# Layer 0's modulation parts 2 to 5: from the head of the work queue to single steps spread among other products

## The chip, the cores and the metric

The kernel runs on one core of a Trainium2 chip. The metric is device time in microseconds (us), here the median of three runs. The core has five engines that each execute their own instruction list in order and wait for each other by semaphores: TensorE (PE, the matrix products, with a second track PEld for loading its stationary operand), VectorE (DVE), ScalarE (ACT), GpSimd (POOL) and SyncE (SP), which issues most of the transfers from memory. Matrix products accumulate in eight banks of PSUM.

## The reference

Two layers (DEPTH = 2) of a diffusion backbone over 256 latent and 256 context tokens, width 1024. Each layer modulates a normalised input by vectors that come from a small product, mixes tokens in three parallel branches, merges them through gates, and runs a gated MLP:

```
def modulation(cvec, w_mod, b_mod):
    m = jax.nn.silu(cvec) @ w_mod + b_mod
    return jnp.split(m[..., None, :], 6, axis=-1)
...
xn = adaln(x, norm1[l], m_lat[0], m_lat[1])
y_lat, y_ctx = token_mixer(xn, hn, ...)        # latent attention, windowed attention, gated delta net
x = x + m_lat[2] * y_lat
x = x + m_lat[5] * conv_ffn(adaln(x, norm2[l], m_lat[3], m_lat[4]), ...)
...
def merge(gates, ya, yb, yc, w_pa, w_pb, w_pc, w_out):
    ga, gb, gc = jnp.split(jax.nn.sigmoid(gates), 3, axis=-1)
    return (ga * (ya @ w_pa) + gb * (yb @ w_pb) + gc * (yc @ w_pc)) @ w_out
```

So parts 0 and 1 of the modulation are needed at once, part 2 only after the output projection, 3 and 4 for the second norm, 5 at the layer's end.

## The kernel before

Both token sets are stacked to 512 columns. Every weight block of 512 KB is loaded into one of three `raw` buffers, split by ScalarE (`wh`, line 189) and VectorE (`wl`, line 179) into a high and a low half, and multiplied in three passes (`mm3`, lines 199 to 201). A unit of `linear` is 256 output columns: two PSUM tiles of 24 products each, in two loads. The tiles come from the tag `mm`, which has three banks (`NMM`); everything else uses the tag `g` with five.

A modulation part (`mod_part`, line 578) is 8 loads of 512 KB, used straight from `raw` with no split: per load 4 matmuls (line 593) into one `mm` tile that stays open for the whole part, and after every second load a yield. So a step is 1 MB and 8 matmuls, a part four steps. Behind the last step the tile is copied out (line 598), transposed (line 601) and added to the bias (line 603). Parts 0 and 1 of layer 0 run at the start of the kernel; layer 1's six run in layer 0's MLP.

The order of layer 0's mixer is set by a queue of generators. A serial chain (the gated delta net's tables, decay, solve and scan; later the two attentions) yields a number at each point where PE would wait for it; `fill` adds the number to a credit, capped at 12, and takes steps from the head of the queue until the credit is used up, each step costing what it yields:

```
self.credit = min(self.credit + us, self.P["cap"])
while self.credit > 0 and self.queue:
    us = next(self.queue[0])
    self.credit -= us
```

The queue is first [q part, v part, kv, gates], later [z, modulation parts 2 and 3] ahead of the gates (`push` puts generators ahead of them), and for the attentions [rotary steps of the windowed attention `gsp`, modulation parts 4 and 5, gates]. A modulation step costs 4.0 in the first place and 0.9 in the second (`modc`). `finish` runs a generator to its end with no credit. The gates are last in the queue: 12 units whose sigmoids go to memory (line 1373) and are read back at the merge (line 1511). A gate unit that has not run when the attentions end is computed in the merge itself (line 1529). A build-time scheduler then sets the final order on each engine, near the order of the calls; `high_priority` moves some of them ahead.

Names that the prediction uses: line 839 is `times_k` (products of keys) in the decay, 877 the first block of the solve, 935, 951, 965, 980 the scan; 1014 the scan's output transposes; 1047, 1094 and 1110 scores, transposes and values of both attentions, 1084 their normalisation; 1248 to 1252 the rotary steps of the windowed attention and 1264 the cast of its keys; 662, 665 and 667 the three reads that take a convolved tile out of its bank; 671 the activation after them and 688 its transposes; 1372 the gates' sigmoid; 1359 z.

Of the kernel before, what the change touches and what calls it, by code (L numbers as in the profile page):

```python
# [29 lines left out]
def make_consts():  # L30
# [56 lines left out]
MARK = None  # L87
P = dict(pw=4,
    l1={}, s2=(2, 1, 2, 0), pe=(0.0, 0.1, 0.0, 0.0), ov=0, np=(0.1, 0.0, 0.25, 0), ly=2, qs=(0, 4), dec1=3.0, dec2=4.0, sol1=4.2, sol2=4.0,
    sol3=1.0, sol4=2.0, sca=(1.0, 2.0), scb=(1.0, 2.0), scc=(1.0, 2.0),   cap=12.0, sl=(0.3, 0.3, 0.5, 0.1), modc=(4.0, 0.9),  # L90
    lag=(0, 0, 2, 4, 5), nmod=(2, 5), hk=(5, 12), f0=(1.0, 1.6, 1.0, 1.0, 1.5, 1.0, 1.0), f1=(1.0, 1.0, 1.0, 0.3, 1.0, 1.0, 0.3), lat=1.0,
    bx=4, wd=0, dc=1, gk=(0, 0), hpe=60, w_t=5, w_k=3, w_s=0, w_r=1.5, w_n=3, w_o=4.0, nr=3, nh=3, nl=4, nb2=7, st=0, ab=(0.0, 0.0, 0.0, 0.0),
    st2=6, bge=2, hpa=40, hpn=0, hpk=40, hpv=40)

_INS = ["x", "c", "ctx", "c_ctx", "w_mod", "b_mod", "norm1", "norm2", "w_in", "mla_q_norm", "mla_kv_norm",
# [39 lines left out]
class Kernel:  # L135
# [67 lines left out]
    def run_gen(self, g):  # L203
        for us in g:
            self.wait = us if isinstance(us, Lat) else 0.0
            self.ahead()
            self.gcount += 1
            if self.bg and self.gcount % self.bg_every == 0:
                try:
                    next(self.bg[0])  # L210
                except StopIteration:
                    self.bg.pop(0)

    def fill(self, us, burst=0.0):

        self.credit = min(self.credit + us, self.P["cap"])
        if self.credit < burst:
            return
        while self.credit > 0 and self.queue:
            if self.wait > 0 and self.queue[0] is not self.gates:  # L220
                self.ahead(1)
            if self.credit <= 0 or not self.queue:
                continue
            try:
                us = next(self.queue[0])
                if isinstance(us, Lat):
                    self.wait = us * self.P["lat"]
                else:
                    self.credit -= us
            except StopIteration:  # L230
                self.queue.pop(0)

    def bg_steps(self):

# [348 lines left out]
    def mod_part(self, l, part, room="raw"):  # L583
# [5 lines left out]
        for k in range(KD):  # L589
            t = self.b4([128, D]) if room == "s4" else self.sb([128, D], "raw", F32, self.NRAW)  # L590
            nc.sync.dma_start(out=t, in_=i["w_mod"][l, k * 128:k * 128 + 128, part * D:part * D + D])
            for q in range(4):
                nc.tensor.matmul(ps[q * 32:q * 32 + 32, :256], lhsT=self.cT[:, k, :], rhs=t[:, q * 256:q * 256 + 256],
                                 start=k == 0, stop=k == KD - 1, tile_position=(0, q * 32))
            if k % 2:
                yield self.modcost
        ev = self.b2([128, 256])
        nc.vector.tensor_copy(ev, ps[:, :256])
        pt = self.ps([128, 4, 128], tag)
# [693 lines left out]
    def layer(self, l):  # L1293
# [113 lines left out]
        self.run_gen(self.gdn_misc(l, X))  # L1407
        gq, gv, gkv, gcq, gsq, gz = self.gdn_part(l, X, 0), self.gdn_part(l, X, 2), proj_kv(), proj_cq(), proj_sq(), proj_z()
        gmk, gmq, go0, go1, gsp = self.mla_kv(l), self.mla_q(l), self.gdn_out(l, 0), self.gdn_out(l, 1), self.swa_prep(l)
        mods = [self.modulation(l, 1), self.modulation(l, 2)]  # L1410
        self.gates = self.gates or gates()
        self.queue = [gq, gv, gkv, self.gates]
        spill = self.dram.tile([128, KD, T], F32, name=f"spill{l}")
# [11 lines left out]
        chain(self.gdn_decay(1, has_q[1]), f=P[f"f{l}"][2])  # L1425
        self.mark(f"gscan_{l}_0")
        alloc_zsq()
        push(*([gz, mods[0]] if l == 0 else [gz, gsq, gcq]))
        if has_q[0]:
            for tl in range(2):  # L1430
                self.times_k(0, tl, 1, self.qk[0][:, tl])
# [25 lines left out]
        nh = 8 // len(qh)  # L1457
        snk = self.sm([128, 8])
        nc.sync.dma_start(out=snk, in_=i["swa_sink"][l].partition_broadcast(128))
        if l == 0:  # L1460
            for _ in self.load_vectors(1):
                pass
            for j in range(DEPTH):
                self.load_conv(j)
        push(*([gsp, mods[1]] if l == 0 else [gsp]))
        self.modcost = self.P["modc"][1]
        ga = self.attend(streams, lambda h: ((qh[h // nh][:, h % nh, :], kh[h // 4][:, h % 4, :]),),
                         lambda h, kt: vt[kt // 2][:, kt % 2, h * 64:h * 64 + 64], lambda u: A["qrs"][:, self.q(u[0] * S, T).start // 128 + u[2]:][:, 0:1], None, False, ya, self.P["sl"][2 * l])
        hs = lambda h: slice((h // 4) * 64, (h // 4) * 64 + 64)
# [24 lines left out]
            self.queue.remove(self.gates)  # L1494
        self.gates = None
        self.finish(*list(self.queue))
        self.modcost = self.P["modc"][0]
        self.tap(f"ya{l}", ya)
        self.tap(f"yb{l}", yb)
        self.tap(f"yc{l}", yc)  # L1500
# [14 lines left out]
        for bi, ((gi, b), y) in enumerate(zip(gate_br, (yc, ya, yb))):  # L1515
# [4 lines left out]
            for u in range(4):  # L1520
# [16 lines left out]
                        nc.gpsimd.tensor_tensor(out=mt, in0=mt, in1=sg[t], op=ALU.add)  # L1537

                self.run_gen(self.linear(i["w_branch_" + b][l], 0, 4, u * 256, 256, yy, ev, cols=lambda _: slice(0, n)))
        self.mark(f"wout_{l}")  # L1540
        mh = [[self.s8([128, 4, n], F32R) for _ in range(2)] for _ in range(2)]
        mH, mL = [[mh[j][k // 4][:, k % 4] for k in range(KD)] for j in range(2)]
# [98 lines left out]
    def run(self):  # L1641
        nc, tc, i = self.nc, self.tc, self.ins
        self.NS8, self.NS4, self.NB2, self.NSM = 8, 9, self.P["nb2"], 32
        self.NRAW, self.NWH, self.NWL, self.NMM = self.P["nr"], self.P["nh"], self.P["nl"], 3
        self.queue, self.bg, self.gcount, self.bg_every, self.credit, self.modcost, self.gates, self.wait, self.sq_last, self.bgx, self.unit, self.wide = [], [], 0, 3, 0.0, 4.0, None, 0.0, None, None, 0, False
        with tc.tile_pool(name="per", bufs=1) as self.per, tc.tile_pool(name="sb", bufs=1) as self.pool, \
                tc.tile_pool(name="psum", bufs=1, space=PSUM) as self.psum, \
                tc.tile_pool(name="dram", bufs=1, space=DRAM) as self.dram:
            self.setup()
            for l in range(DEPTH):  # L1650
                self.layer(l)
            self.mark("final")
            self.final()
# [62 lines left out]
```

## Time and profile before

| | us |
|---|---|
| median of 3 runs | 1779.97 (1774.64 to 1780.54) |
| profiled execution, its own time | 1780.76 |
| span of its instructions | 1779.0 |
| PE, records of matmuls | 1679.0 (94%) |
| VectorE busy | 1133.4 (64%) |
| ScalarE busy | 769.2 (43%) |
| GpSimd busy | 300.4 (17%) |
| mean granted PE clock | 0.968 of full |

Busy PE means that a matmul's record is open. At half clock the records are longer, so a stretch can read as fully busy and still lose time; the granted clock beside it tells. The profile follows one execution, and a wait for several semaphores is put down to the one that came last.

### The profile page before, as it was taken

To read this page: it belongs to the slowest core of one execution; us is meant where nothing else is said; L and a number is where in the kernel's file an instruction comes from. 1 tells how busy PE (TensorE), PEld (TensorE's weight loads), DVE (VectorE), ACT (ScalarE), POOL (GpSimd) and SP (SyncE) were. 2 spreads that over 40 slices of the span, in tenths; PEclk is the share of its full clock that TensorE was granted. 3 is DMA by queue.
4 is the path that set the end of the run, shared out by engine and by line. 5 is a ranking of instruction groups with operands and counts; after the bars stand their busy time and mean duration, and the time that the engine had idled before them with its cause. 6 is when DMAs were issued, how large, how long until landed. Compare 5 with 4: busy or idle time off the path is not lost. (4 is left out here: it accounts for less than half of the span.)

```text
span 1779.0 us, 31557 instructions
## 1 busy us (share of the span) xinstructions
PE 1679.0 (94%) x12723; PEld 1363.7 (77%) x12723; DVE 1133.4 (64%) x2159; ACT 769.2 (43%) x1371; POOL 300.4 (17%) x281
## 2 busy tenths in 40 slices
PE   7989988999999999999999999999898899999997
PEld 4768765776556888768888888778787667999997
DVE  3897595474865643545535553699796776677684
ACT  3644312233755333324313432464523475555463
POOL 1040411221200222001100112030502310213010
PEclk8999998998999999999999999999998999999999
DMA  9423326333043633663333343434352223745663
GB/s 346 115 72 107 96 73 190 72 75 111 25 143 122 210 119 120 253 231 96 98 95 103 95 141 120 125 92 141 90 120 58 60 77 98 236 144 182 185 185 124
DMA packets 216944, 228.75 MB, mean 129 GB/s; under 512 B 51228, under 2 KB 195422, under 8 KB 215646
## 3 DMA queue, kind: packets, MB, share of 16 engines
q1 hardware_dynamic: 211582, 220.11, 40.5%
q10 hardware_dynamic: 4928, 6.56, 1.0%
q8 instruction: 100, 1.64, 0.4%
q14 instruction: 46, 0.38, 0.1%
q0 software_dynamic: 288, 0.06, 0.0%
HBM read 213.85 MB, written 11.80 MB: 127 GB/s over the span
## 5 line engine op out<-in xcount | busy, mean ns | idle before, releaser
L179 DVE TENSOR_TENSOR wl<-raw,wh 128x1024 fp32r<-128x1024 f32 (+2 forms) x294 | 364.3, 1239 | 250.2 <-ACT wh L189 248.6
L189 ACT CAST wh<-raw 128x1024 fp32r<-128x1024 f32 (+2 forms) x294 | 298.4, 1017 | 422.3 <-PE mm L200 220.5
L199 PE MATMUL mm<-xnh,wh 128*128 128x512 f32 (+2 forms) x1072 | 380.3, 356 | 5.8 <-ACT wh L189 2.4
L201 PE MATMUL mm<-xnh,wl 128*128 128x512 f32 (+2 forms) x1072 | 375.9, 353 | 1.3 <-DVE wl L179 1.3
L200 PE MATMUL mm<-xnl,wh 128*128 128x512 f32 (+2 forms) x1072 | 376.0, 351 | 0.1
L199 PEld LDWEIGHTS mm<-xnh,wh 128*128 128x128 f32 (+1 forms) x1072 | 206.3, 193 | 39.4 <-issue 7.0
L201 PEld LDWEIGHTS mm<-xnh,wl 128*128 128x128 f32 (+1 forms) x1072 | 205.9, 192 | 31.5 <-issue 3.3
L200 PEld LDWEIGHTS mm<-xnl,wh 128*128 128x128 f32 (+1 forms) x1072 | 206.1, 192 | 27.8 <-issue 2.9
L199 PE MATMUL g<-xnh,wh 128*128 128x256 f32 (+1 forms) x496 | 167.3, 340 | 1.4 <-ACT xnh L405 1.4
L200 PE MATMUL g<-xnl,wh 128*128 128x256 f32 (+1 forms) x496 | 166.4, 337 | 0.2 <-DVE xnl L406 0.2
L201 PE MATMUL g<-xnh,wl 128*128 128x256 f32 (+1 forms) x496 | 166.1, 336 | 0.0
L201 PE MATMUL mm<-s,wl 128*128 128x256 f32 (+1 forms) x458 | 150.0, 328 | 0.6 <-DVE wl L179 0.6
L199 PE MATMUL mm<-s,wh 128*128 128x256 f32 (+1 forms) x458 | 150.1, 329 | 0.4 <-DVE s L534 0.3
L200 PE MATMUL mm<-s,wh 128*128 128x256 f32 (+1 forms) x458 | 149.6, 327 | 0.1
L1616 POOL TENSOR_TENSOR b<-b,b 128x512 f32<-128x512 f32 (+1 forms) x44 | 54.3, 1234 | 442.5 <-DVE b L1600 381.6
L199 PEld LDWEIGHTS g<-xnh,wh 128*128 128x128 f32 x496 | 94.6, 192 | 15.0 <-issue 3.3
L199 PE MATMUL g<-s,wh 128*128 128x512 f32 (+1 forms) x304 | 102.8, 338 | 0.0
L201 PEld LDWEIGHTS g<-xnh,wl 128*128 128x128 f32 x496 | 94.6, 191 | 10.5 <-issue 1.2
L200 PEld LDWEIGHTS g<-xnl,wh 128*128 128x128 f32 x496 | 94.7, 191 | 10.1 <-DVE xnl L406 0.8
L200 PE MATMUL g<-s,wh 128*128 128x512 f32 (+1 forms) x304 | 102.2, 336 | 0.0
L201 PE MATMUL g<-s,wl 128*128 128x512 f32 (+1 forms) x304 | 102.2, 336 | 0.0
L199 PEld LDWEIGHTS mm<-s,wh 128*128 128x128 f32 x458 | 87.2, 191 | 8.8 <-DVE s L534 1.1
(285 smaller groups left out, 2743.6 us busy)
## 6 DMA issues: line engine op xcount, KB each, us to landing
raw<-in_w_in_dram SPq DMA_DIRECT2D x92, 512.0 KB
raw<-in_ffn_up_dram SPq DMA_DIRECT2D x80, 512.0 KB
s<-in_w_mod_dram SPq DMA_DIRECT2D x64, 512.0 KB
raw<-in_w_mod_dram SPq DMA_DIRECT2D x32, 512.0 KB
raw<-in_ffn_down_dram SPq DMA_DIRECT2D x32, 512.0 KB
raw<-in_w_out_dram SPq DMA_DIRECT2D x16, 512.0 KB
raw<-in_ffn_down_dram SPq DMA_DIRECT2D x16, 384.0 KB
spill<-s SPq DMA_DIRECT2D x4, 1024.0 KB
```

Source lines behind the costliest of these rows:

```text
L179: self.nc.vector.tensor_tensor(out=out, in0=x, in1=h.bitcast(F32), op=ALU.subtract)
L189: nc.scalar.copy(H, raw)
L199: mm(ps, lhsT=wH, rhs=xH, start=start, stop=False)
L200: mm(ps, lhsT=wH, rhs=xL, start=False, stop=False)
L201: mm(ps, lhsT=wL, rhs=xH, start=False, stop=stop)
L1616: nc.gpsimd.tensor_tensor(out=y[:, cs], in0=y[:, cs], in1=av[t][:, cs], op=ALU.mult)
```

## The change

The two generators for parts 2 and 3 and for 4 and 5 of layer 0 no longer stand in the queue. They form a list of their own, `drip`. Every product step that yields, in the queue or run to its end by `run_gen`, adds its yield to a counter (`drop`); at 14.0 the counter is reset and one modulation step is taken, which costs 1.0 of credit. What is left when the merge is done is run before the output projection.

```
-    scc=(1.0, 2.0),   cap=12.0, sl=(0.3, 0.3, 0.5, 0.1), modc=(4.0, 0.9),
+    scc=(1.0, 2.0),   cap=12.0, sl=(0.3, 0.3, 0.5, 0.1), modc=1.0,
...
-    bx=4, wd=0, dc=1, ...
+    bx=4, drip=14.0, wd=0, dc=1, ...
...
         for us in g:
             self.wait = us if isinstance(us, Lat) else 0.0
             self.ahead()
+            self.drop(us)
...
                     self.credit -= us
+                    self.drop(us)
...
+    def drop(self, us, every=None):
+
+        self.dropped += us
+        if self.drip and self.dropped >= (self.P["drip"] if every is None else every):
+            self.dropped = 0.0
+            try:
+                self.credit -= next(self.drip[0])
+            except StopIteration:
+                self.drip.pop(0)
...
             if k % 2:
-                yield self.modcost
+                yield self.P["modc"]
...
-        mods = [self.modulation(l, 1), self.modulation(l, 2)]
+        if l == 0:
+            self.drip = [self.modulation(l, 1), self.modulation(l, 2)]
...
-        push(*([gz, mods[0]] if l == 0 else [gz, gsq, gcq]))
+        push(*([gz] if l == 0 else [gz, gsq, gcq]))
...
-        push(*([gsp, mods[1]] if l == 0 else [gsp]))
-        self.modcost = self.P["modc"][1]
+        push(gsp)
...
+        while self.drip:
+            self.drop(0.0, 0.0)
         self.mark(f"wout_{l}")
```

In the new program the lines behind the change have other numbers: 593 is 605, 980 is 992, 935 is 947, 1084 is 1096, 1251 and 1252 are 1263 and 1264, 1264 is 1276.

On PE, in the scan of group 0 behind the last z product (`mm_2232`), the order before was this, with scan blocks (lines 965, 980, 935) between the modulation's matmuls:

```order
L201 MATMUL mm_2232<-xnh_227,wl_2272 128x512
L593 MATMUL mm_2347<-raw_2348,cT 32x256 x4
L593 MATMUL mm_2347<-raw_2354,cT 32x256 x4
L965 MATMUL g_2364<-b_351_2360,s_45_263 64x64 x8
L965 MATMUL g_2374<-b_351_2360,s_45_263 64x64 x8
L593 MATMUL mm_2347<-raw_2390,cT 32x256 x4
L980 MATMUL g_2404<-b_357_2402,s_142_769 64x64 x16
L935 MATMUL g_2422<-b_328_2152,s_49_267 64x64 x3
L593 MATMUL mm_2347<-raw_2396,cT 32x256 x4
```

In the changed program the last z product there (`mm_2376`) is followed by gate products (`mm_2516`), with one step of 8 modulation matmuls among them:

```order
L201 MATMUL mm_2376<-xnh_227,wl_2440 128x512
L199 MATMUL mm_2516<-xnh_227,wh_2520 128x512
L200 MATMUL mm_2516<-xnl_228,wh_2520 128x512
L201 MATMUL mm_2516<-xnh_227,wl_2521 128x512
...
L605 MATMUL mm_1580<-raw_2530,cT 32x256 x4
L605 MATMUL mm_1580<-raw_2536,cT 32x256 x4
L199 MATMUL mm_2516<-xnh_227,wh_2520 128x512
L200 MATMUL mm_2516<-xnl_228,wh_2520 128x512
```

Two whole parts in a row have become one step, and gate products have taken their place. The tile `mm_1580` of part 3 had been opened long before.

On GpSimd, in the latent attention, the rotary steps of the windowed attention (lines 1251 and 1252) stood between the attention's normalisations (line 1084) before:

```order
L1084 TENSOR_SCALAR b_623_4158<-b_623_4158,sm_4144 128x256
L1251 TENSOR_TENSOR s_238_1398<-s_238_1398,cst 128x256
L1252 TENSOR_TENSOR s_238_1398<-s_238_1398,b_636_4191 128x256
L1251 TENSOR_TENSOR s_544_3783<-s_544_3783,cst 128x256
L1252 TENSOR_TENSOR s_544_3783<-s_544_3783,b_649_4225 128x256
L1084 TENSOR_SCALAR b_646_4216<-b_646_4216,sm_4197 128x256
```

In the changed program they come behind the last of those normalisations, the one of 512 columns, and the casts of the keys (line 1276) behind them all:

```order
L1096 TENSOR_SCALAR b_744_4674<-b_744_4674,sm_4655 128x256
L1096 TENSOR_SCALAR b_808_4862<-b_808_4862,sm_4857 128x512
L1263 TENSOR_TENSOR s_245_1435<-s_245_1435,cst 128x256
L1264 TENSOR_TENSOR s_245_1435<-s_245_1435,b_847_5012 128x256
L1263 TENSOR_TENSOR s_593_4110<-s_593_4110,cst 128x256 x2
L1264 TENSOR_TENSOR s_593_4110<-s_593_4110,b_849_5018 128x256
...
L1264 TENSOR_TENSOR s_593_4110<-s_593_4110,b_855_5036 128x256
L1276 CAST s_858_5047<-s_858_5047 64x512 x2
```

All ten rotary instructions and the two casts now form one block at the boundary of the two attentions.

## Rows read from the trace of the kernel before

**Rows 1.** The page, part 1: busy us, share of the span, instructions.
```profile
PE 1679.0 (94%) x12723; PEld 1363.7 (77%) x12723; DVE 1133.4 (64%) x2159; ACT 769.2 (43%) x1371; POOL 300.4 (17%) x281
```

**Rows 2.** Busy by stretch: length, busy by engine (instructions), granted clock, DMA share, GB/s.
```profile
64.80:85.90 21.10, 20.81 (x103) 16.35 (x101) 18.23 (x57) 11.21 (x20) 0.00 (x0) 1.00 0.33 81
85.90:190.40 104.50, 98.68 (x485) 79.44 (x485) 78.86 (x158) 49.20 (x92) 21.27 (x18) 0.97 0.32 95
190.40:219.70 29.30, 28.82 (x413) 22.02 (x412) 17.92 (x21) 11.38 (x16) 20.66 (x17) 1.00 0.32 94
219.70:304.10 84.40, 69.26 (x963) 50.83 (x962) 61.51 (x131) 15.84 (x23) 8.28 (x8) 0.90 0.42 133
304.10:388.00 83.90, 80.99 (x1089) 62.07 (x1088) 46.82 (x90) 26.16 (x42) 17.71 (x19) 0.96 0.29 69
388.00:433.60 45.60, 39.84 (x195) 30.30 (x196) 23.28 (x57) 12.09 (x22) 9.59 (x9) 0.94 0.32 80
433.60:564.10 130.50, 123.98 (x676) 75.56 (x676) 94.08 (x282) 89.40 (x229) 14.64 (x17) 0.94 0.30 96
564.10:674.90 110.80, 110.80 (x498) 90.63 (x497) 53.00 (x59) 34.44 (x46) 23.19 (x15) 1.00 0.51 168
```

**Rows 3.** Waits from 219.7 to 304.1: who waited for whom, us, times, longest.
```profile
PEld mm L593 <- DMA raw<-in_w_mod_dram: 7.2, 8, 1.5
PE mm L593 <- DMA raw<-in_w_mod_dram: 5.8, 8, 1.3
```

**Rows 4.** Busy by stretch inside stage 3, columns as in rows 2.
```profile
220.00:230.00 10.00, 5.62 (x152) 5.29 (x152) 7.03 (x10) 3.80 (x5) 3.62 (x4) 0.66 0.15 57
...
240.00:250.00 10.00, 10.00 (x72) 8.15 (x71) 9.38 (x24) 1.20 (x2) 0.50 (x1) 1.00 0.18 56
...
270.00:280.00 10.00, 8.68 (x168) 5.62 (x172) 5.99 (x19) 1.27 (x4) 0.00 (x0) 0.83 0.77 230
...
290.00:304.10 14.10, 12.41 (x96) 9.16 (x94) 6.11 (x9) 4.19 (x4) 0.00 (x0) 0.76 0.45 134
```

**Rows 5.** Line 199 alone in the merge: length, PE busy, PEld busy, clock, DMA.
```profile
564.10:609.60 45.50, 24.06 (x62) 11.48 (x62) 1.00 0.66 223
609.60:674.90 65.30, 37.34 (x96) 18.04 (x97) 1.00 0.41 130
```

**Rows 6.** PE in order of time: start, length, line, tiles, shape.
```profile
278.75 0.64 PE L593 MATMUL mm<-raw,cT 128*32 128x256 f32 x8
279.31 1.02 PE L935 MATMUL g<-b,s 64*64 64x64 f32 x36
```

**Rows 7.** Transfers by line: layer 0's gate stores.
```profile
gates<-b ACTq DMA_DIRECT2D x16, 256.0 KB
```

**Rows 8.** PE, VectorE and ScalarE in order of time, 102 to 117.
```profile
102.22 0.39 PE L201 MATMUL mm<-xnh,wl 128*128 128x512 f32 x1
...
113.17 0.53 PE L688 MATMUL g<-cst,s 128*128 128x128 f32 x2 [3.54 <-ACT s L671]
...
111.96 0.75 DVE L667 SCALAR_TENSOR_TENSOR b<-mm,vec,b 128x510 f32<-128x510 f32 x1
...
116.73 0.60 ACT L1372 ACTIVATE b<-mm 128x512 f32<-128x512 f32 x1 [0.75 <-PE mm L201]
```

**Rows 9.** Busy by stretch inside the attentions, columns as in rows 2.
```profile
433.60:440.00 6.40, 6.40 (x28) 3.86 (x29) 3.72 (x14) 3.65 (x10) 0.00 (x0) 0.50 0.65 240
...
454.50:476.00 21.50, 21.28 (x108) 11.71 (x106) 20.18 (x51) 19.30 (x44) 4.46 (x6) 1.00 0.08 26
...
524.00:564.10 40.10, 40.10 (x215) 25.67 (x215) 25.97 (x78) 28.77 (x69) 0.00 (x0) 1.00 0.28 88
```

**Rows 10.** GpSimd's groups from 441 to 464: busy us, mean ns, idle before.
```profile
L1252 POOL TENSOR_TENSOR s<-s,b 128x256 f32<-128x256 f32 x5 | 3.6, 726 | 1.8 <-DVE b L1250 1.6
L1251 POOL TENSOR_TENSOR s<-s,cst 128x256 f32<-128x256 f32 x5 | 3.2, 637 | 3.8 <-PE g L1248 3.8
L1264 POOL CAST s<-s 64x512 fp32r<-64x512 f32 x2 | 2.0, 978 | 2.8 <-ACT s L1263 2.7
```

More of the change, by code (lines that the diff above doesn't have):

```diff
@@ L89 @@
     l1={}, s2=(2, 1, 2, 0), pe=(0.0, 0.1, 0.0, 0.0), ov=0, np=(0.1, 0.0, 0.25, 0), ly=2, qs=(0, 4), dec1=3.0, dec2=4.0, sol1=4.2, sol2=4.0,
-    sol3=1.0, sol4=2.0, sca=(1.0, 2.0), scb=(1.0, 2.0), scc=(1.0, 2.0),   cap=12.0, sl=(0.3, 0.3, 0.5, 0.1), modc=(4.0, 0.9),
+    sol3=1.0, sol4=2.0, sca=(1.0, 2.0), scb=(1.0, 2.0), scc=(1.0, 2.0),   cap=12.0, sl=(0.3, 0.3, 0.5, 0.1), modc=1.0,
     lag=(0, 0, 2, 4, 5), nmod=(2, 5), hk=(5, 12), f0=(1.0, 1.6, 1.0, 1.0, 1.5, 1.0, 1.0), f1=(1.0, 1.0, 1.0, 0.3, 1.0, 1.0, 0.3), lat=1.0,
-    bx=4, wd=0, dc=1, gk=(0, 0), hpe=60, w_t=5, w_k=3, w_s=0, w_r=1.5, w_n=3, w_o=4.0, nr=3, nh=3, nl=4, nb2=7, st=0, ab=(0.0, 0.0, 0.0, 0.0),
+    bx=4, drip=14.0, wd=0, dc=1, gk=(0, 0), hpe=60, w_t=5, w_k=3, w_s=0, w_r=1.5, w_n=3, w_o=4.0, nr=3, nh=3, nl=4, nb2=7, st=0, ab=(0.0, 0.0, 0.0, 0.0),
     st2=6, bge=2, hpa=40, hpn=0, hpk=40, hpv=40)
@@ L1496, in layer @@
         self.finish(*list(self.queue))
-        self.modcost = self.P["modc"][0]
         self.tap(f"ya{l}", ya)
@@ L1644, in run @@
         self.NRAW, self.NWH, self.NWL, self.NMM = self.P["nr"], self.P["nh"], self.P["nl"], 3
-        self.queue, self.bg, self.gcount, self.bg_every, self.credit, self.modcost, self.gates, self.wait, self.sq_last, self.bgx, self.unit, self.wide = [], [], 0, 3, 0.0, 4.0, None, 0.0, None, None, 0, False
+        self.queue, self.bg, self.gcount, self.bg_every, self.credit, self.gates, self.wait, self.sq_last, self.bgx, self.unit, self.wide, self.drip, self.dropped = [], [], 0, 3, 0.0, None, 0.0, None, None, 0, False, [], 0.0
         with tc.tile_pool(name="per", bufs=1) as self.per, tc.tile_pool(name="sb", bufs=1) as self.pool, \
```

## The prediction

> **What bounds the kernel now.** I read the page's busy time first [rows 1]: TensorE (PE) has records for 1679.0 of 1779.0 us. So nothing that only hides work behind PE can help; a gain must come from time in which PE waits or runs at its half clock. Then I cut layer 0's mixer at PE instructions that stand in both programs and asked for a table by stage [rows 2]. The cuts are: the first product of the q part (64.8), the first block of the solve (line 877, 190.4), the block of 64 of line 839 that ends the decay of group 1 (219.7), the second solve's block of line 877 (304.1), the first output transpose of group 0 (line 1014, 388.0), the first scores (line 1047, 433.6), the last transpose of probabilities (line 1094, 564.1), the first output-projection product (674.9). I call them stages 1 (the first two rows) to 7.
>
> The reader is to see two losses in each row: length minus PE busy, and (1 minus PEclk) times the length, which is what is lost where the clock is at the lower of its two levels (1.2 instead of 2.4 GHz). They are: stage 1 6.1 + 3.1; stage 2 0.5 + 0; stage 3 15.1 + 8.4; stage 4 2.9 + 3.4; stage 5 5.8 + 2.7; stage 6 6.5 + 7.8; stage 7 nothing. That is 62 us in all, 24 of it in stage 3, where the queue's head is the modulation: PE there stands 5.8 us before modulation matmuls, for their weights (the weight-load row beside it, 7.2, is the same time seen by PE's other half) [rows 3], and the clock is 0.83 from 270 and 0.76 from 290, behind the last of them [rows 4]. The same stage also starts badly, at 0.66 with PE busy 5.62 of 10 us [rows 4]: line 839 waits for VectorE there, not for modulation.
>
> **What the change moves.** All 16 steps stay (8 matmuls, 1 MB each), so PE's work is the same to the instruction; what changes is its place. Two prices are needed. A product of 512 columns: the last four merge units hold 96 of line 199, so 288 products, in 65.3 us [rows 5], 0.2267 us each. A modulation matmul: 8 records (4 instructions) start 0.56 us before what follows [rows 6], 0.14 us each, 18 us for all 128.
>
> The order shows more than the steps' move. They cost the queue 4.0 credit each in the scan and now 1.0, so the scan's filler becomes gate products: ScalarE issues 24 gate stores in layer 0 instead of 16 [rows 7], which means all 12 gate units are done before the attention or in its first microseconds, and none is left for the merge. Counted in the order, by stage, after minus before:
> - stage 1: 24 gate products fewer, 40 modulation matmuls more: +0.2 us of PE work
> - stage 2: 24 products and 8 matmuls more: +6.6
> - stage 3: 108 products more, 40 matmuls fewer: +18.9
> - stage 4: 40 products and 16 matmuls more: +11.3
> - stage 5: 81 products and 8 matmuls more: +19.5
> - stage 6: 33 products and 32 matmuls fewer: -12.0
> - stage 7: 196 products fewer: -44.4
>
> The sum is nil, as it must be. So the time changes by what the 62 us of losses do.
>
> Stage 7 is PE at full clock with no idle, so its 44.4 are gained whole. Behind it, a merge unit without gates is one load and one gate read back per 5.5 us; that is how its first eight units run already, 45.5 us at 223 GB/s [rows 5].
>
> Stages 2 and 3 take 25.5 and have 24 of losses. The 5.8 of DMA waits go with the burst, and so do the slow clock in and behind it (0.17 of 10 and 0.24 of 14.1 us, 5.1) and the 1.7 that PE then idles for the first gate's weights [rows 4]: 12.6, of which I take 12. The bad start costs 4.4 idle and up to 3.4 by the clock; stage 2's 6.6 us of new work stand ahead of it, and I take 4 of the 7.8. So 16 saved, between 0 (fill only delays the chain) and 24: nearer the upper end, because VectorE has room, 61.5 of 84.4 us busy [rows 2], for the four or five splits that the extra loads add. Net +9.5.
>
> Stage 4: 1.0 saved (0 to 6.3), net +10.3: PE was busy 81.0 of 83.9 us. Stage 5: the 37 gate products that now stand before the first scores replace the modulation's first 16 matmuls, and the clock of 0.50 that follows them in the row from 433.6 [rows 9] suggests that stretch was thin. 4.5 of 8.5 saved (0 to 8.5), net +15.0.
>
> Stage 6 loses its filler. From 524.0 on PE is busy 40.1 of 40.1 us at full clock, so what leaves there is gained; from 454.5 VectorE is at 20.2 and ScalarE at 19.3 of 21.5 [rows 9], so nothing can be gained there. And there is a new wait. With the queue's credit spent on gates, the rotary steps of the windowed attention no longer run inside the latent attention: GpSimd's ten of them now stand behind its last normalisation, as the order shows, and the casts of the keys behind those. At 0.637 + 0.726 us five times and 0.978 twice [rows 10] that is 8.8 us which the first windowed scores wait for, less what drains beside it. I take 8.5 of the 12 gained after that wait (bounds: 12, and -2 with the whole wait and a lower clock).
>
> Stage 1: the steps there hold one of three accumulator banks from the first step until each part's end, so a pair of products has two banks, not three. A gate's evacuation takes 0.60 us [rows 8], and the other tile's 12 products (2.7 us) cover it. A convolved tile's takes longer: its last product started at 102.22 and took 0.39, its last reader started at 111.96 and took 0.75, so 10.1 us lie between their ends [rows 8]. PE stood 3.54 us at 113.17 behind the same chain [rows 8], so most of it is paid already: I take 1.5 (bounds -1 and 15: 10.1 less the 2.7 covered, for two pairs). Layer 1: the credit left over differs, and 25 gate products of 256 columns move from inside its attention to before it. Half of 0.2267 times 25 is 2.8: between -3 and +3, I take +1.3.
>
> By the Trainium skill (Perfetto Trace Analysis, section Matmuls) independent groups should rotate through different PSUM banks so that one's evacuation runs beside the next one's matmuls. Holding a bank through most of stages 1 to 6 goes against that; by it the 1.5 of stage 1 would be 15 or more. The gate's 0.60 us against 2.7 of cover says it does not bind there; for the convolved tiles the trace agrees with it.
>
> Sum: 1.5 + 9.5 + 10.3 + 15.0 - 8.5 - 44.4 + 1.3 = -15.3. The profiled execution took 1780.8 (its span and 1.8 around it), 0.8 above the median of the runs shown: 1780.0 - 15 = 1765.
>
> **Rivals.**
> 1. Filler hides whole. VectorE's chain in stage 3 has 22.9 us of slack, and PE was full in stage 4 already while its chain went on, which speaks for it. Stages 2 to 5, with 56.3 of new work, then keep 6 of 39 us of loss, and the windowed attention's new wait drains beside the old one: 56.3 - 33 - 12 - 44.4 + 1 = -32, 1748. Against it: the chain's own gaps, such as the start of stage 3, are not modulation's.
> 2. PE is in order, so each chain instruction stands behind more products and the chain is late by as much. Only the DMA waits go (5.8 of 24), and stages 4 and 5 save 1: 6.8 saved in place of 21.5, so 1780. For it: in stage 3's first half VectorE is the one that is full (9.38 of 10 us from 240) [rows 4], and a delay there is passed on. Against: in stage 4 PE lost only 6.3 of 83.9 us under dense filler.
> 3. Slower: the held bank. Place: the convolved pairs of stage 1 (192 products, four pairs). If every next pair's tile waits for a 10.1 us evacuation less the 2.7 covered, 7.4 four times, that is 30 us in place of 1.5: 1793. It decides from the point where VectorE's backlog outlasts 2.7 us and PE has no other instruction to go to. For it: VectorE is busy 78.9 of 104.5 us there. Against: the wait at 113.17 is paid already, and gates and projections leave by one short copy. The Trainium skill's rule on PSUM banks is this rival's.
>
> **How the numbers follow.** Forecast 0.60, with a range of its own from 1755 to 1774; rival 1 0.15 (1744 to 1755); rival 2 0.15 (1774 to 1785); rival 3 0.10 (1786 up). A measurement of this kernel can tell about 0.3%, 5.3 us, from no change. Faster than 1774.6: the forecast, rival 1 and nothing else, 0.75. Within: rival 2, 0.15. Slower: rival 3, 0.10. Range for 8 in 10: from inside rival 1 to the middle of rival 2, 1750 to 1780.
>
> **What would show it.** The stage table again: stage 1 near 127 us, 2 and 3 together near 123, 4 near 94, 5 near 61, 6 near 122, 7 near 66. No wait of modulation matmuls for DMA over 3 us in all. In stage 7 no sigmoid of a gate. Between the two attentions, GpSimd's rotary rows in one block and PE idle for 5 to 9 us before the first windowed scores. It is wrong if stages 2 and 3 grow by 25 us (rival 2), if stage 1 grows by over 10 with PE waiting for VectorE's lines 665 and 667 (rival 3; 12 lines later in the new program), or if stage 6 grows.

## The result and the profile after

The changed kernel is slower: 1796.3 us (median of four runs, 1795.2 to 1797.9) against 1780.0, a ratio of 1.0094 with a 95% interval from 1.0073 to 1.0115. The prediction was 1765, faster. The page's first row answers to [rows 1]; PE's instructions are the same 12723, its records 15 us longer:

```profile
PE 1694.0 (94%) x12723; PEld 1369.6 (76%) x12723; DVE 1140.3 (64%) x2159; ACT 771.0 (43%) x1373; POOL 300.0 (17%) x281
```

The same cuts as in [rows 2], stage 1 in one row, and behind them two rows more: from the output projection to layer 1, and layer 1 up to its own output projection. Columns as there: length, busy by engine (instructions), granted clock, DMA share, GB/s.

```profile
64.50:201.40 136.90, 122.67 (x646) 93.84 (x644) 100.43 (x209) 58.28 (x108) 22.50 (x18) 0.95 0.38 115
201.40:237.30 35.90, 35.80 (x454) 26.95 (x452) 19.35 (x25) 16.86 (x22) 21.37 (x18) 1.00 0.39 124
237.30:331.40 94.10, 84.97 (x989) 66.49 (x988) 64.03 (x130) 21.48 (x30) 7.21 (x7) 0.95 0.36 105
331.40:427.60 96.20, 92.11 (x1166) 70.72 (x1163) 49.51 (x94) 26.50 (x41) 20.06 (x20) 0.95 0.37 97
427.60:489.50 61.90, 59.27 (x295) 45.54 (x293) 27.24 (x63) 18.18 (x29) 7.84 (x7) 0.97 0.53 134
489.50:625.10 135.60, 122.12 (x572) 72.52 (x570) 92.73 (x276) 86.56 (x226) 15.19 (x17) 0.81 0.15 48
625.10:692.20 67.10, 67.10 (x309) 54.38 (x307) 38.63 (x49) 20.38 (x29) 19.66 (x13) 1.00 0.61 199
692.20:1190.50 498.30, 488.96 (x2646) 395.10 (x2644) 248.95 (x381) 179.44 (x276) 56.32 (x49) 0.99 0.43 139
1190.50:1560.80 370.30, 346.18 (x3557) 291.14 (x3558) 308.49 (x629) 193.74 (x354) 89.96 (x88) 0.95 0.37 102
```

The last two of before:

```profile
674.90:1167.10 492.20, 486.65 (x2646) 394.12 (x2644) 245.37 (x376) 177.83 (x274) 52.83 (x47) 1.00 0.43 136
1167.10:1545.00 377.90, 344.85 (x3558) 289.99 (x3559) 303.20 (x629) 191.26 (x352) 92.47 (x88) 0.95 0.36 100
```

| change of length, us | forecast | profile |
|---|---|---|
| stage 1 | +1.5 | +11.3 |
| stages 2 and 3 | +9.5 | +16.3 |
| stage 4 | +10.3 | +12.3 |
| stage 5 | +15.0 | +16.3 |
| stage 6 | -8.5 | +5.1 |
| stage 7 | -44.4 | -43.7 |
| output projection and MLP | 0 | +6.1 |
| layer 1 | +1.3 | -7.6 |
| sum | -15.3 | +16.0 |

The large terms came out within 2 us: the gates leave the merge whole, and stages 4 and 5 pay for them. Five others did not. The reader is to see their marks in the rows: stage 1 idles 14.2 us instead of 6.1; stages 2 and 3 still lose 13.9 us to idle time and clock, of 24.0 before; stage 6's clock is 0.81 instead of 0.94, by which it loses 25.8 us (1 minus the clock, times the length) against 7.8; the row behind the merge idles 9.3 instead of 5.6 at a clock below 1; layer 1 is shorter with the same work.

Who PE waits for in stage 1 (us, times, longest), before and after:

```profile
PE g L688 <- ACT s L671: 3.5, 1, 3.5
PE g L839 <- DVE s L809: 2.1, 1, 2.1
```

```profile
PE mm L199 <- DVE b L679: 4.9, 4, 2.8
PE g L700 <- DVE s L131: 4.8, 1, 4.8
PE g L783 <- DVE gtb L765: 1.9, 1, 1.9
PE mm L605 <- DVE mod L615: 1.9, 1, 1.9
```

Line 679 is the last reader of a convolved tile (667 before) and 199 the first product of another tile: four times PE waits for a bank, which it did not do in this stage before. The last row is a modulation step that waits for the tile of the part before. ScalarE shows the other half. It makes the high half of a weight block, and now waits for blocks to land, 11 times for 38.5 us in all; the kernel before has no such wait in stage 1. I take the reason to be that the raw buffers hold modulation, which kernel own_s4 below tests. One of them:

```profile
185.68 1.05 ACT L189 CAST wh<-raw 128x1024 fp32r<-128x1024 f32 x1 [5.21 <-DMA raw<-in_w_in_dram]
```

In stages 2 and 3 the waits for modulation's weights [rows 3] are gone; the one at the start stays and is longer (6.4 us before line 851, where it was 4.3 before line 839):

```profile
PE g L851 <- DVE s L131: 6.4, 1, 6.4
PE g L963 <- DVE b L952: 2.8, 1, 2.8
```

In stage 6 the wait for the casts of the keys stands where it was expected, 4.9 us:

```profile
PE g L1106 <- DVE sm L131: 5.3, 3, 2.9
PE g L1059 <- POOL s L1276: 4.9, 1, 4.9
```

What follows was not expected: half clock for some 50 us. From 579 to 599 PE is full while VectorE is at 5.35 and 4.70 of 10 and ScalarE at 4.75 and 4.61, so by these records PE itself, at half clock, is the bound there. In [rows 9] the same attention from 524.0 had 1.00.

```profile
549.00:559.00 10.00, 5.70 (x18) 2.91 (x18) 8.77 (x16) 5.88 (x13) 4.58 (x5) 0.59 0.29 101
559.00:569.00 10.00, 7.65 (x26) 4.63 (x26) 6.89 (x28) 6.17 (x23) 0.00 (x0) 0.50 0.00 1
569.00:579.00 10.00, 8.97 (x29) 5.02 (x28) 6.45 (x22) 4.59 (x15) 0.00 (x0) 0.50 0.00 0
579.00:589.00 10.00, 10.00 (x30) 5.45 (x30) 5.35 (x21) 4.75 (x17) 0.00 (x0) 0.50 0.00 0
589.00:599.00 10.00, 10.00 (x30) 5.48 (x31) 4.70 (x16) 4.61 (x13) 0.00 (x0) 0.50 0.01 2
599.00:609.00 10.00, 10.00 (x51) 6.13 (x49) 6.67 (x21) 6.12 (x15) 0.00 (x0) 0.85 0.00 1
```

Behind the merge PE waits for the sum's last tiles to be split (line 194), 3.1 us, and GpSimd's additions show why:

```profile
PE g L199 <- ACT s L194: 3.1, 2, 2.8
```

```profile
682.36 1.30 POOL L1548 TENSOR_TENSOR s<-s,s 128x512 f32<-128x512 f32 x1 [2.11 <-issue]
685.78 2.14 POOL L1548 TENSOR_TENSOR s<-s,s 128x512 f32<-128x512 f32 x1 [2.12 <-DVE s L1547]
690.03 1.29 POOL L1548 TENSOR_TENSOR s<-s,s 128x512 f32<-128x512 f32 x1 [2.11 <-issue]
```

They repeat every 7.67 us for two tiles, while a merge unit of 24 products takes PE 24 times 0.2267, 5.4. VectorE multiplies, GpSimd adds, ScalarE rounds, VectorE takes the rest, and only then multiplies the next tile. So each of the last units falls some 2 us behind PE.

### The profile page after: what moved, and what is told of

It reads as the page before. It is cut to its first block, busy times and chain, and to the rows that moved or that the text cites. A ratio compares the mean times of both kernels' runs of the same rounds, so it can differ in the third digit from the quotient of the medians.

```text
span 1794.7 us, 31592 instructions
## 1 busy us (share of the span) xinstructions
PE 1694.0 (94%) x12723; PEld 1369.6 (76%) x12723; DVE 1140.3 (64%) x2159; ACT 771.0 (43%) x1373; POOL 300.0 (17%) x281
## 5 line engine op out<-in xcount | busy, mean ns | idle before, releaser
L179 DVE TENSOR_TENSOR wl<-raw,wh 128x1024 fp32r<-128x1024 f32 (+2 forms) x294 | 367.7, 1251 | 256.7 <-ACT wh L189 255.2
L199 PE MATMUL mm<-xnh,wh 128*128 128x512 f32 (+2 forms) x1136 | 409.4, 361 | 11.7 <-DVE b L679 4.9
L201 PE MATMUL mm<-xnh,wl 128*128 128x512 f32 (+2 forms) x1136 | 400.3, 354 | 1.5 <-DVE wl L179 1.4
L200 PE MATMUL mm<-xnl,wh 128*128 128x512 f32 (+2 forms) x1136 | 401.4, 354 | 0.2
L200 PEld LDWEIGHTS mm<-xnl,wh 128*128 128x128 f32 (+1 forms) x1136 | 219.4, 193 | 29.4 <-issue 2.9
L199 PE MATMUL g<-xnh,wh 128*128 128x256 f32 (+1 forms) x432 | 142.7, 333 | 1.4 <-ACT xnh L417 1.4
L200 PE MATMUL g<-xnl,wh 128*128 128x256 f32 (+1 forms) x432 | 141.5, 329 | 0.2 <-DVE xnl L418 0.2
L201 PE MATMUL g<-xnh,wl 128*128 128x256 f32 (+1 forms) x432 | 141.4, 329 | 0.0
L199 PE MATMUL g<-s,wh 128*128 128x512 f32 (+1 forms) x320 | 109.7, 343 | 3.1 <-ACT s L194 3.1
L200 PE MATMUL g<-s,wh 128*128 128x512 f32 (+1 forms) x320 | 109.3, 342 | 0.4 <-DVE s L195 0.4
L1059 PE MATMUL g<-s,s 96*128 96x512 f32 (+3 forms) x192 | 92.1, 545 | 5.3 <-POOL s L1276 4.9
L199 PEld LDWEIGHTS g<-xnh,wh 128*128 128x128 f32 x432 | 82.7, 192 | 12.4 <-issue 3.3
L201 PEld LDWEIGHTS mm<-s,wl 128*128 128x128 f32 x442 | 85.6, 194 | 7.3 <-issue 0.4
```

The lines of the kernel that those rows point to most:

```text
L179: self.nc.vector.tensor_tensor(out=out, in0=x, in1=h.bitcast(F32), op=ALU.subtract)
L199: mm(ps, lhsT=wH, rhs=xH, start=start, stop=False)
L200: mm(ps, lhsT=wH, rhs=xL, start=False, stop=False)
L201: mm(ps, lhsT=wL, rhs=xH, start=False, stop=stop)
L1059: nc.tensor.matmul(p[:, :nk], lhsT=a[:, self.q(q0, q0 + 128)], rhs=b[:, :nk], start=j == 0, stop=j == len(ops) - 1 and not (mask and st == 1))
```

## The experiments

Each was timed in five rounds beside the kernel before on the same chip, so its ratio is a safer comparison than its median. Two pairs give the scatter of a stage between profiles: kernel l1credit below has the kernel before's instructions ahead of layer 1, and its stages differ by up to 2.5 us; kernel vecm has the changed kernel's ahead of the merge's third branch, and differs by up to 3.0. The stages are those of one profiled execution, which is not always near the median: 7.1 us above it in credit_only, 5.7 in own_s4, 3.8 in own_bank and hold_late10, 2.5 below it in l1credit and 9.1 below in hold_late_q. The stages of all:

| us | median | ratio to before | 1 | 2+3 | 4 | 5 | 6 | 7 | MLP | layer 1 |
|---|---|---|---|---|---|---|---|---|---|---|
| before | 1780.0 | | 125.6 | 113.7 | 83.9 | 45.6 | 130.5 | 110.8 | 492.2 | 377.9 |
| changed | 1796.3 | 1.0094 | 136.9 | 130.0 | 96.2 | 61.9 | 135.6 | 67.1 | 498.3 | 370.3 |
| own_bank | 1783.9 | 1.0031 (1.0017 to 1.0046) | 131.3 | 132.4 | 102.8 | 56.4 | 132.1 | 64.4 | 496.0 | 371.3 |
| own_s4 | 1779.2 | 1.0008 (0.9990 to 1.0027) | 126.7 | 135.8 | 101.2 | 58.1 | 128.5 | 67.3 | 496.6 | 372.1 |
| late | 1798.0 | 1.0098 (1.0078 to 1.0117) | 125.4 | 125.9 | 86.6 | 61.6 | 140.3 | 87.9 | 493.6 | 377.4 |
| gsp_early | 1791.0 | 1.0080 (1.0060 to 1.0100) | 134.6 | 131.2 | 99.8 | 64.9 | 125.9 | 67.1 | 498.0 | 368.3 |
| vecm | 1789.8 | 1.0063 (1.0043 to 1.0083) | 135.3 | 130.9 | 96.7 | 61.9 | 138.6 | 67.0 | 491.5 | 368.2 |
| gates8 | 1807.4 | 1.0171 (1.0149 to 1.0194) | 134.6 | 130.5 | 78.8 | 55.5 | 125.1 | 109.1 | 491.7 | 382.1 |
| hold4 | 1787.0 | 1.0043 (1.0028 to 1.0059) | 135.0 | 130.6 | 78.8 | 57.5 | 121.2 | 92.8 | 491.9 | 379.2 |
| credit_only | 1809.3 | 1.0187 (1.0163 to 1.0212) | 125.6 | 147.4 | 98.4 | 48.5 | 140.4 | 75.8 | 497.9 | 382.9 |
| l1credit | 1769.9 | 0.9943 (0.9921 to 0.9966) | 125.5 | 113.3 | 81.4 | 44.0 | 130.5 | 110.8 | 492.3 | 370.2 |
| three | 1770.0 | 0.9943 (0.9921 to 0.9966) | 126.3 | 131.8 | 101.6 | 61.1 | 121.6 | 67.3 | 489.4 | 372.1 |
| hold_late10 | 1769.2 | 0.9949 (0.9931 to 0.9966) | 125.5 | 133.0 | 70.8 | 56.0 | 121.5 | 101.2 | 491.8 | 373.5 |
| hold_late_q | 1776.5 | 0.9987 (0.9966 to 1.0008) | 125.5 | 131.3 | 71.3 | 49.2 | 125.9 | 104.0 | 491.5 | 367.4 |

**Stage 1: the bank and the buffers.** own_bank:

```
- bufs={"mm": self.NMM, "g": 8 - self.NMM}[tag]
+ bufs={"mm": self.NMM, "md": 1, "g": 7 - self.NMM}[tag]
- tag = "g" if room == "s4" else "mm"
+ tag = "g" if room == "s4" else "md"
```

> The changed kernel with one edit: a modulation tile that stays open gets a PSUM bank of its own (a tag md with one bank; the tag g has four instead of five), so the products keep all three mm banks. Theory A (the held bank makes stage 1 longer: PE waits for the readers of convolved tiles, line 679, 4.9 us, and for what stands behind them): stage 1 falls from 136.9 us to about 127, total about 1786. Theory B (it is the 1 MB loads, which take the raw buffers and the transfers from the products' weights): stage 1 stays within 2 us of 136.9 and the total at 1796, or above by what the missing g bank costs the scan and the attentions.

own_s4 adds to it:

```
- t = self.b4([128, D]) if room == "s4" else self.sb([128, D], "raw", F32, self.NRAW)
+ t = self.b4([128, D])
```

> Kernel own_bank with one more edit: the dripped steps load into buffers of the tag s4 (nine of 512 KB, which hold other tensors of the mixer) and not into the three raw buffers of the products' weights. So neither a bank nor a raw buffer is taken. own_bank: stage 1 131.3 us and 1784; kernel late, with no modulation in stage 1: 125.4. Theory A (what own_bank leaves of stage 1's loss is the raw buffers): stage 1 125 to 127 us, total 1778 to 1781, if the steps do not wait for s4 buffers elsewhere. Theory B (it is the steps' place in PE's order and the transfers themselves): 130 to 132, total 1783 to 1786.

late puts no modulation into stages 1 and 2:

```
- self.drip = [self.modulation(l, 1), self.modulation(l, 2)]      (behind the small projections)
+ self.drip, self.dropped = [self.modulation(l, 1), self.modulation(l, 2)], 0.0   (behind alloc_zsq)
```

> The changed kernel with one edit: the list of dripped parts is filled at the scan of group 0 and not after the small projections, so stages 1 and 2 hold no modulation step (and 24 more gate products, as in the kernel before). own_bank took back 5.6 of the 11.4 us of stage 1. Theory A (the rest is the 1 MB loads, which take raw buffers from the products' weights): stage 1 is 125.5 us as before, and the total 1783 to 1787. Theory B (what stage 1 loses is only passed on, since the gate products that leave it then stand in stage 3): stage 1 is 125.5, but stages 2 to 4 take it back and the total is 1791 to 1796.

Stage 1 of the three, in this order:

```profile
65.40:196.70 131.30, 120.31 (x646) 92.84 (x644) 97.97 (x209) 57.93 (x108) 21.92 (x18) 0.97 0.40 118
```

```profile
63.40:190.10 126.70, 120.92 (x646) 92.46 (x644) 97.00 (x214) 58.59 (x108) 18.98 (x16) 0.97 0.42 126
```

```profile
64.00:189.40 125.40, 120.52 (x588) 96.70 (x586) 97.03 (x213) 60.53 (x111) 21.30 (x18) 0.96 0.33 92
```

In own_bank PE's wait for the readers of convolved tiles has fallen from 4.9 us to one of 1.6, and in own_s4 it is gone, as are ScalarE's waits for weight blocks:

```profile
PE mm L199 <- DVE b L679: 1.6, 1, 1.6
```

Both theories of own_bank were half right. Against the changed kernel's 136.9 the bank is 5.6 of the 11.3 us. But gsp_early, vecm, gates8 and hold4 run the same PE instructions in stage 1 as the changed kernel, and it took 134.6 to 135.3 us there; so stage 1 grew by 9.0 to 11.3, and the bank is 3.3 to 5.6 of it. The raw buffers are another 4.6, and with both free the 40 modulation matmuls cost stage 1 nothing that can be told. Not all of it stays gained: stages 2 and 3 are 3.4 us longer in own_s4 than in own_bank. The medians give more than the stage, 12.4 us for the bank's edit and 4.7 for the buffers' (11.2 and 4.1 by the ratios). Part of the rest is stage 6, shorter by 3.5 and 7.1 us than the changed kernel's, for which the next section has a reason. late frees the whole of stage 1 and gains nothing in all, for another reason than either theory had: a drip that starts late isn't done in time. Seven steps were left for the end of the merge, and PE waited there for their transfers:

```profile
PE mm L605 <- DMA raw<-in_w_mod_dram: 8.3, 5, 5.8
```

Its stages 1 to 5 are 25.5 us shorter than the changed kernel's, its stages 6 and 7 25.5 us longer.

**Stage 6: the wait, or the filler.** gsp_early:

```
- push(gsp)
+ self.run_gen(gsp) if l == 0 else push(gsp)
```

> The changed kernel with one edit: layer 0's rotary steps of the windowed attention are run to their end ahead of the latent attention, not as filler or at the boundary. The same work, so the wait of 4.9 us for the keys' casts goes. Theory A (the half clock of 50 us in the windowed attention, 0.50 from 559 to 599, follows from that wait): the clock there is near 1.00 again, the windowed attention falls from 72.4 to about 60 us, total 1796 - 13 = 1783. Theory B (the clock falls because the attention has no filler left): the clock stays at 0.5 for tens of us, only the wait goes, total 1791 to 1793. A slow result, over 1796, would say that PE waits for the rotary steps at the head of the latent attention instead.

The wait is gone, stage 6 is 9.7 us shorter, of which stages 4 and 5 take back 6.6 (partly scatter). Yet the half clock came all the same, with no long wait ahead of it:

```profile
554.00:564.00 10.00, 8.94 (x37) 5.30 (x35) 6.85 (x31) 6.53 (x25) 0.00 (x0) 0.79 0.01 2
564.00:574.00 10.00, 8.97 (x30) 4.78 (x26) 5.98 (x22) 4.85 (x17) 0.00 (x0) 0.50 0.00 0
574.00:584.00 10.00, 10.00 (x30) 5.49 (x30) 5.35 (x20) 4.43 (x17) 0.00 (x0) 0.50 0.00 0
584.00:594.00 10.00, 10.00 (x29) 5.21 (x29) 4.81 (x17) 4.92 (x14) 0.00 (x0) 0.50 0.00 0
```

So theory A falls: the wait of 4.9 us isn't needed for it. hold4 gives the attentions filler, products of the queue that run between the steps of the attention's own chain:

```
+ if l == 0:
+     self.finish(*[g for g in self.queue if g is self.gates])
+     self.gates = gates((2, 3))          # units 8 to 11; the queue held 0 to 7
+     self.queue.append(self.gates)
  push(gsp)
```

> The changed kernel with one edit: the last four gate units of layer 0 are held back until the attentions begin, and are their filler; those that have not run go to the merge. By the order the attentions then hold 55 gate products in place of 11 (14.7 us of filler in place of 7.5). Theory A (the half clock in the windowed attention comes from the lack of filler): its clock is over 0.9 and stage 6 is no longer than 136 us though it holds 7 us more; the wait for the keys' casts may stay. Theory B (it comes from that wait): a half clock for 30 us or more stays behind it. The total goes with kernel gates8 (1807, which it resembles in stages 4 and 5): by theory A 1795 to 1803, by B 1806 to 1812.

```profile
465.70:586.90 121.20, 114.53 (x604) 69.58 (x602) 90.97 (x275) 88.00 (x228) 14.71 (x17) 0.99 0.18 59
```

The clock is 0.99, and stage 6 is 14.4 us shorter than in the changed kernel though it holds 7 us more filler. Theory A of this run held, and the total was better than it said. Here the rotary steps also ran earlier, without a wait at the boundary of the two attentions, so the two runs show that the wait isn't needed for the half clock and that filler with no wait prevents it.

The other traces bear on the case between, filler with the wait left in, though none has the filler right at the boundary. In own_bank the wait is there (4.9 us), the clock fell at 551.3, a tile of 12 products ran from 572.9 to 582.0, and the half clock ended at 578.8:

```profile
558.00:568.00 10.00, 7.10 (x20) 4.43 (x19) 8.31 (x29) 4.80 (x18) 0.00 (x0) 0.50 0.01 2
568.00:578.00 10.00, 10.00 (x30) 6.06 (x30) 6.48 (x21) 6.53 (x23) 0.00 (x0) 0.50 0.00 0
578.00:588.00 10.00, 10.00 (x50) 5.89 (x49) 6.13 (x25) 5.19 (x19) 0.00 (x0) 0.97 0.00 0
```

In own_s4 (with the wait), gates8 and three (without it) the clock also came back amid such filler, after 27.5, 13.5 and 17.0 us. In the changed kernel, vecm and late (with the wait) and gsp_early (without) no product came until the clock had risen by itself, and it was half for 37 to 58 us. Where the filler stands also counts. credit_only has 48 modulation matmuls in stage 6 and yet a clock of 0.80: none of them runs in the first 29 us after the fall at 543.3, and behind the first 16 that follow the clock falls again. The kernel before and hold_late_q have as many in stage 6, 32 of them near the boundary, and 0.94 and 0.95. And a held clock isn't all of it: three's stage 6, at 0.90 and with 24 products less than hold4's, takes 121.6.

**The gates.** gates8 leaves the last four units to the merge (`gate_br[:2]` in layer 0); credit_only is the kernel before with `modc=(1.0, 0.9)` and 1.0 to begin with.

> The changed kernel with one edit: layer 0's queue holds 8 gate units, not 12; the last four are computed in the merge, as in the kernel before. The drip stays. Theory A: stage 1 stays near 137 us (held bank), stage 7 is about 108 again, the output projection no longer waits for the merge's last sums (6 us less in what follows stage 7), the attention has even less filler: 1786 to 1794. Theory B (the moved gates are the whole loss): 1780, as the kernel before. If it is over 1797, the gates that ran ahead were a gain that the other losses hid.

> The kernel before with one edit: a modulation step costs 1.0 of credit in the scan and 0.9 in the attentions, in place of 4.0 and 0.9. No drip: parts 2 to 5 stay the queue's first in one burst each. All 12 gate units then run ahead of the merge, as in the changed kernel, with no open modulation tile in stage 1. Theory A (the loss is the held bank in stage 1, about 11 us, with the attention without filler and the merge without gates, about 11 more): stage 1 is 125.5 as before, stage 6 has 10.8 us of filler in place of 19.4, the output projection waits as in the changed kernel: 1780 to 1788. Theory B (moving gates is the whole loss): as slow as the changed kernel, 1794 to 1798. Theory C (gates moved are a gain, and only the drip spoils it): below 1770.

Both were slower than I thought, and the totals mislead: against the changed kernel layer 1 is 11.8 and 12.6 us longer in them. I take that to be the credit that layer 0 leaves over (kernel l1credit, below); for these two it was not tested. So each is read from layer 0 alone. gates8's 11 us are all layer 1: keeping four units for the merge is neither gain nor loss in layer 0 (mixer +5.9, the stretch behind the merge -6.6). Against hold4, where by the order two of the four units run beside stages 5 and 6, its stage 7 is 16.3 us longer, and stages 5 and 6 are no shorter for it (180.6 and 178.7). Up to hold4's amount, work beside the attentions was free, and in the merge it was paid whole.

credit_only has nearly the changed kernel's gates and the old bursts. Its layer 0, to the end of the MLP, is 32 us longer than before's. Against the changed kernel the mixer is 8.4 us longer: 11.3 won in stage 1, 19.7 lost behind it. So the credit that brings the gates forward costs by itself. In stage 3 the spread steps win some of that back; whether anything is left of it over the whole mixer is not shown, since this profiled execution is 7.1 us above its median. Stage 3 with a burst and 138 gate products:

```profile
219.60:337.40 117.80, 100.55 (x1070) 72.26 (x1070) 65.85 (x134) 24.15 (x33) 8.36 (x8) 0.86 0.42 131
```

That is 17.2 idle and 16.5 lost by the clock, against 9.1 and 4.7 in the changed kernel's 94.1 us with as many gate products.

**The merge's chain.** vecm:

```
- nc.gpsimd.tensor_tensor(out=mt, ...)
+ (nc.vector if l == 0 and bi == 2 else nc.gpsimd).tensor_tensor(out=mt, ...)
```

> The changed kernel with one edit: in the third branch of layer 0's merge VectorE, not GpSimd, adds the gated product to the sum (8 additions of 128x512). Theory A (with gates read back a merge unit has 5.45 us of products, but its chain VectorE, GpSimd, ScalarE, VectorE takes 7.66 us for two tiles, and the output projection waits at its end for 3.5 us and at half clock for the same again): the chain is shorter by GpSimd's 1.3 to 2.1 us each, the wait goes, the stretch from the output projection to layer 1 is 492 instead of 498 us, total 1790. Theory B (the wait is the last tile's latency, which any order of engines has): 497, total 1796.

498.3 became 491.5 us, PE waits for no split any more in the 20 us behind the merge, and the total fell by 6.5 (5.5 by the ratios), as theory A said.

**Layer 1.** l1credit is the kernel before with one line at the start of layer 1:

```
+ self.credit -= 0.86
```

> The kernel before with one edit: at the start of layer 1 the credit is lowered by 0.86, from -1.60 to the -2.46 that the changed kernel has there, which gives layer 1 nearly the changed kernel's order of work. Layer 0 is untouched. Theory A (the 7.6 us that layer 1 is shorter in the changed kernel come from that order and have nothing to do with modulation): layer 1 takes 370 instead of 378 us, total 1779 - 7.5 = 1771, faster than both. Theory B (they are scatter between two profiled executions): 1779.

```profile
1161.80:1532.00 370.20, 344.99 (x3557) 289.71 (x3558) 308.13 (x629) 193.98 (x354) 91.22 (x88) 0.96 0.37 102
```

Layer 1 is 370.2 us, as in the changed kernel, and the kernel before becomes faster, by 0.57%. The gain of 7.6 us was an accident of the credit that layer 0 leaves over, and has nothing to do with modulation. (Layer 0 was 5 us shorter in this profile too, with the same instructions; that is scatter.)

**Together.** three has own_s4, vecm and gsp_early:

> The changed kernel with three edits of runs before together: the modulation's tile and loads out of the products' bank and raw buffers (own_s4, -17), VectorE's additions in the third branch of the merge (vecm, -6.5) and the rotary steps ahead of the latent attention (gsp_early, -5.3). Theory A (three separate losses, which add): 1796 - 29 = 1767, with stage 1 near 127 us, stage 6 near 122 and 492 us from the output projection to layer 1. Theory B (the half clock of the windowed attention stays, for want of filler, and takes back what the rotary steps gain): stage 6 128 us or more, 1772 to 1778.

```profile
62.90:189.20 126.30, 120.52 (x646) 92.22 (x644) 97.08 (x214) 58.59 (x108) 19.00 (x16) 0.97 0.43 126
483.70:605.30 121.60, 113.61 (x550) 65.81 (x548) 88.65 (x269) 85.92 (x225) 12.39 (x14) 0.90 0.10 33
672.60:1162.00 489.40, 484.52 (x2646) 393.99 (x2644) 246.50 (x377) 178.33 (x274) 50.77 (x46) 1.00 0.43 139
```

26.3 us of the 28.9 that the three gained alone: they are separate losses and nearly add. hold_late10 is late, hold4, `drip=10.0` and `self.credit = -2.46` at layer 1; hold_late_q drips only parts 2 and 3 and has 4 and 5 in the queue at the attentions.

> What the runs point to, together: the changed kernel with the drip filled at the scan of group 0 (late) and one step each 10 us in place of 14, the last four gate units held back for the attentions (hold4), and the credit set to -2.46 at the start of layer 1 (l1credit). By stages, from the runs: 125.4, 29.2 and about 96 for stages 1 to 3 (late), 78 and 56 for stages 4 and 5 (hold4 with 1 us less filler), 121 for stage 6 (hold4), 98 for stage 7 (91.5 of work and some waiting for four steps run in a row), 492, 370 and 233.5 behind it, 64 ahead: 1763. If terms do not add, because what one stage gains is lost in the next, it ends at 1772 or above, no better than l1credit (1770).

> As hold_late10, but only parts 2 and 3 are dripped; parts 4 and 5 stand in the queue at the attentions as in the kernel before. No step is left for the end of the merge. By stages: 125.4, 29.2, 96, 78, 50 (29 us of filler), 123 (14.9 us of filler, 48 modulation matmuls and 36 gate products), 102, 492, 370, 233.5, 64 ahead: 1763. Theory A (steps in a row at the end of the merge cost their transfers): faster than hold_late10 by about 3. Theory B (modulation is poorer filler for the attentions than gate products, as in credit_only): its stage 6 has a half clock for 20 us or more and is over 130 us, total 1770 or above.

hold_late10 beats both kernels, and so do three and l1credit, all within a microsecond of 1769.5. hold_late10 missed its sum by 6. Stage 3 took 103.5 us instead of 96, with 40 modulation matmuls in it and not late's 24, but stage 4 gave that back (70.8 instead of 78). What is left in the profile is stage 7 (101.2 instead of 98) and layer 1 (373.5 instead of 370). hold_late_q is 7 us slower by the median, against its theory A. Theory B can't be judged: stage 6 took 125.9 us, but in an execution of 1767.4. Its executions run from 1766 to 1781, the three below 1770 at a mean granted clock of 0.972 to 0.976 and the others at 0.960 to 0.967, and in which stage the clock differs isn't shown. What matters: with layer 1's accident given to both, the best drip (1769.2) and no drip at all (l1credit, 1769.9) are the same.

## Why the prediction was wrong

**Right.** The order's consequences: gates out of the merge (-43.7 for -44.4), stages 4 and 5 (+12.3 and +16.3 for +10.3 and +15.0), the DMA waits of [rows 3] gone, the block of rotary steps at the boundary with a wait of 4.9 us. Two of the marks that were to show it wrong then decided: stage 1 grew by 11.3 us (9.0 to 9.7 in the four kernels with the same order) with PE waiting for the readers of convolved tiles, and stage 6 grew.

**Stage 6, 13.6 us, the largest miss (16.6 in vecm, which has the same instructions there).** The step was "I take 8.5 of the 12 gained after that wait (bounds: 12, and -2 with the whole wait and a lower clock)". It took PE's full clock from 524.0 as a property of the attention. It hung on filler at the boundary of the two attentions: without it the clock halves, by gsp_early with no wait needed, and PE becomes the bound; with it hold4 kept 0.99. The lower bound of -2 had the word clock in it but priced only a few us of it; the row from 433.6 with 0.50 [rows 9], read as a thin stretch in stage 5, was the price to use.

**Stage 1, 9.8 us.** "I take 1.5 (bounds -1 and 15)". The bank cost 3.3 to 5.6 (own_bank). Its cover was the other tile's 2.7 us, and four times PE came to the end of that. What wasn't in the sum at all is the raw buffers: a step takes two of three, 4.6 us (own_s4). I had counted its matmuls and its bank, and not the buffers that its 1 MB passes through. Part of that goes through VectorE: a split starts when its block has landed, and three splits between 97 and 113 us ran beside GpSimd and took 3.26, 2.06 and 3.03 us, where no split of stage 1 took over 1.3 in the kernel before (the last section has the reason). own_bank has two such splits and own_s4 one; how much of the loss is theirs isn't shown. Rival 3 named the right place and end; its 30 us stand against at most 5.6 for the bank, and that its total of 1793 came near 1796 is chance, made up by the buffers, stage 6 and the merge. By the Trainium skill (Perfetto Trace Analysis, section Matmuls) independent groups should rotate through different banks; the trace agrees, with PE's wait for the convolved tiles' readers down from 4.9 to 1.6 us for one bank given back.

**Stages 2 and 3, 6.8 us.** "I take 12" for the burst and "4 of the 7.8" for the start. Idle and clock together fell from 24.0 to 13.9, so 10 and not 16: the burst's part came, but the start's wait grew from 4.3 to 6.4 us. The work put ahead of it didn't shorten this wait for VectorE.

**The merge, 6.1 us.** "That is how its first eight units run already" read a unit's length off units of the first two branches. The third branch also splits the sum, and its chain of 7.67 us per unit outlasts 5.4 of products (vecm). Before, the 48 products of a gate in each of those units hid it.

**Layer 1, 8.9 us the other way.** "Between -3 and +3": priced by the work that moved, where what counted was what idles. Without it the change would have cost some 24 us.

Not shown: why the start of stage 3 waits longer, whether a held bank alone, with the buffers free, costs as much, and whether the wait for the keys makes the half clock longer.

## What to carry to other kernels

Before work is taken out of a stage, ask what its absence does to the clock there: filler beside a latency-bound chain can be free, and it can hold the clock that the chain's own matmuls run at. Look where in the chain it stands, and not only how much of it there is. Of a moved step count every shared thing that it occupies and for how long (bank, load buffer, queue), not only its instructions. And where an order comes from a running counter, look at what the edit leaves in that counter: here 0.86 of leftover credit took as much off the kernel before as the best of the kernels that were meant to be faster.

## What the runs showed of the hardware

GpSimd's addition of 128x512 took 1.29 us or 2.14, in turn. The long ones overlap a split by VectorE:

```profile
685.55 1.22 DVE L179 TENSOR_TENSOR wl<-raw,wh 128x1024 fp32r<-128x1024 f32 x1
```

It began at 685.55 and ended at 686.77, and GpSimd's addition, from 685.78, ended at 687.92, 1.15 us after it. It goes the other way too. The split took 1.2 us on average from 144 to 201, and 2.8 from 94 to 114, where GpSimd was busy for 15.1 of 20 us:

```profile
L179 DVE TENSOR_TENSOR wl<-raw,wh 128x1024 fp32r<-128x1024 f32 x9 | 11.0, 1223 | 15.9 <-ACT wh L189 15.9
```

```profile
L179 DVE TENSOR_TENSOR wl<-raw,wh 128x1024 fp32r<-128x1024 f32 x3 | 8.4, 2786 | 0.0
```

By the Trainium skill (SBUF — State Buffer, section Who interferes with whom) a VectorE instruction with two SBUF inputs and a GpSimd instruction that reads SBUF block each other, the later one until the first is done. The trace agrees: from the moment at which the split ends the addition runs for 1.15 us, near its own 1.29.
